# Inverting the gated-DeltaNet blocks in 16x16 pieces over 128 partitions, with one more merge on the tensor engine

## The chip, the cores and the metric

The kernel runs on one core of a Trainium2 chip. The metric is the device time of one execution in microseconds (us), the median of several runs of the same program. The engines of the core are named as the profile names them: PE (TensorE, the matmul engine) with PEld (its weight loads), DVE (VectorE), ACT (ScalarE), POOL (GpSimd) and SP (SyncE, which here only starts transfers). ACT also starts transfers; ACTq and SPq are the rows of those two queues.

## The reference, cut to what matters

One decoder layer over 2048 tokens of width 1024: a norm, an input projection that feeds three mixers (a convolution module, a gated DeltaNet with 4 heads of 64, differential attention), an output projection, and a SwiGLU network of width 2816. The part that the change touches is one triangular solve in the DeltaNet mixer, for every chunk of 64 tokens and every head:

```python
lower = jnp.where(strict, beta[..., None] * kk * decay, 0.0)
a_mat = lower + jnp.eye(c, dtype=jnp.float32)          # c = 64, unit lower triangular
...
sol = lax.linalg.triangular_solve(a_mat, rhs, left_side=True, lower=True, unit_diagonal=True)
u_c, w_c = sol[..., :dv], sol[..., dv:]
...
def step(state, inp):                                  # one step per chunk, in order
    v_new = u_i - jnp.einsum('bhcd,bhde->bhce', w_i, state)
    ...
```

There are 32 chunks and 4 heads, so 128 such 64x64 triangular matrices.

## The kernel before, in words

The 2048 tokens are worked on in four units of 512 (u = 0 to 3). A first phase runs, unit by unit, everything that needs the input projection. The order of its steps is written out by hand in one string: I is the DeltaNet's input projection with its short convolution, G the DeltaNet proper (`gdn_unit`), C the taps of the long convolution, L its norm, K and V the projections of attention, N the norm of the next unit, A the attention of unit 0. A planner then places the instructions of all engines with costs of its own and with priorities (`hp`); every engine then runs its own list strictly in that order. After the first phase come the attention of the other units, the output projection and the feed-forward network, in one long stream of matmuls. Large matmuls are done three times (`mm3`: high x high, high x low, low x high) and their weights go through three buffers `wp`, loaded by SP.

`gdn_unit` (L430) has 32 matrices in a unit (4 heads x 8 chunks). It forms the lower triangles L (L435 to L456), stores them to DRAM (`gL`, L457) and reads the two diagonal 32x32 blocks of each back with one block per partition: 64 partitions, 32x32 numbers each (`Lg`, L463). DVE then inverts all 64 blocks at once by substitution: 31 steps of two instructions, an outer product (L470) and a subtraction from the rows below (L472). The inverses `Tt` and their transposes go back to DRAM (`gT`, L474, L475) and are read again in the layout of the tokens: the transposes into the diagonal of `X64` (L480), the first block untransposed into `T1` (L483). Two rounds of small matmuls on PE make the 32x32 block beside the diagonal: `yp` (L490) and, after a copy on ACT (L495), `wp` (L500), which ACT writes into `X64` (L503). PE's fp32 matmul appears in the trace as two instructions, so that the 32 matmuls of `yp` in a unit are 64 instructions, and the same for `wp`. Then a scan over the 8 chunks of the unit (L528 to L581) uses `X64` at L522 and L542 and carries the state `Sbd` (L562) from chunk to chunk and from unit to unit. All of its accumulators and those of the merge share two PSUM banks, the tags "sc" and "o".

The transfers of `gL`, `Lg`, `gT`, `X64` and `T1` are all started by ACT. SP starts the loads of weights (L114, L118). A tile's tag names its place in memory: tiles of one tag follow each other in the same place. The pools p1 and gd end with the first phase, and the tiles of the feed-forward phase (pool `pa`) take over gd's place once all its tiles are done with, the last of them those of the scan of unit 3 and of a first part of the output projection (`hx`, L1016 to L1023).

Of the kernel before, what the change touches and what calls it, by code (L numbers as in the profile page):

```python
# [10 lines left out]
F32 = mybir.dt.float32  # L11
F32R = mybir.dt.float32r
AF = mybir.ActivationFunctionType
ALU = mybir.AluOpType
# [33 lines left out]
def body(ctx: ExitStack, tc: tile.TileContext, x, norm1_g, w_in, conv_dw_w, conv_dw_b,  # L48
# [16 lines left out]
    gL = [dram.tile([H, U, C], F32, name=f"gL{u}", tag=f"gL{u}") for u in range(NU)]  # L65
    gT = [dram.tile([2, 2, H, 8, 32, 32], F32, name=f"gT{u}", tag=f"gT{u}") for u in range(NU)]

# [5 lines left out]
    def cst(shape, name):  # L73
        return const.tile(shape, F32, name=name, tag=name)
# [172 lines left out]
    V.memset(Sbd, 0.0)  # L247
    X64 = cst([P, H, TU, C], "X64")
    V.memset(X64, 0.0)
    hist4 = cst([P, 6, 3], "hist4")  # L250
# [179 lines left out]
    def gdn_unit(u, qtok, sc):  # L430
        L, QKT = sc["L"], sc["QKT"]

        def qkh(tt):
            return qtok[:, tt, 0:512].rearrange("p (h d) -> p h d", d=C)
        for tt in range(TU):  # L435
# [10 lines left out]
            for hp in range(2):  # L446
# [8 lines left out]
                for d_, b in ((L, 0), (QKT, 1)):  # L455
                    V.tensor_tensor(d_[:, hp::2, tt, :], kv[:, :, b, :], d_[:, hp::2, tt, :], op=ALU.mult)  # L456
        nc.scalar.dma_start(gL[u].rearrange("h (t p) c -> p (h t) c", p=P), L.rearrange("p h t c -> p (h t) c"))  # L457

        Lg = gd.tile([64, 32, 32], F32, name=f"Lg{u}", tag="Lg")
        Tt = gd.tile([64, 32, 32], F32, name=f"Tt{u}", tag="Tt")  # L460
        for blk in range(2):
            b0 = blk * 32
            nc.scalar.dma_start(Lg[b0:b0 + 32], gL[u].rearrange("h (c r) s -> (h c) r s", c=8)[:, b0:b0 + 32, b0:b0 + 32])  # L463
        V.memset(Tt, 0.0)
        V.memset(Tt.rearrange("p a b -> p (a b)")[:, 0:1024:33], 1.0)
        for j in range(31):
            n = 31 - j
            tm = gd.tile([64, 256], F32, name=f"tm{u}_{j}", tag="tg")
            tv = tm[:, 0:n * (j + 1)].rearrange("p (a b) -> p a b", a=n)
            V.tensor_tensor(tv, Lg[:, j + 1:, j:j + 1].to_broadcast([64, n, j + 1]),  # L470
                            Tt[:, j:j + 1, 0:j + 1].to_broadcast([64, n, j + 1]), op=ALU.mult)
            V.tensor_tensor(Tt[:, j + 1:, 0:j + 1], Tt[:, j + 1:, 0:j + 1], tv, op=ALU.subtract)  # L472
        V.tensor_copy(Lg, Tt.rearrange("p a b -> p b a"))
        nc.scalar.dma_start(gT[u][0].rearrange("k h c a b -> (k h c) a b"), Tt)  # L474
        nc.scalar.dma_start(gT[u][1].rearrange("k h c a b -> (k h c) a b"), Lg)  # L475
        T1 = gd.tile([P, H, TU, 32], F32, name=f"T1_{u}", tag="Lg")
        for ch in range(2):
            for blk in range(2):
                r0 = ch * C + blk * 32
                nc.scalar.dma_start(  # L480
                    X64[r0:r0 + 32, :, :, blk * 32:blk * 32 + 32].rearrange("p h t c -> p (h t) c"),
                    gT[u][1, blk].rearrange("h (t c) s q -> c s (h t) q", c=2)[ch])
            nc.scalar.dma_start(T1[ch * C:ch * C + 32].rearrange("p h t c -> p (h t) c"),  # L483
                              gT[u][0, 0].rearrange("h (t c) s q -> c s (h t) q", c=2)[ch])

# [110 lines left out]
    def conv_ln(u, acc2):  # L596
# [22 lines left out]
        for ct in range(2):  # L619
            yl = acc2[:, ct, :]  # L620
            ty = gd.tile([P, U], F32, name=f"cy{u}_{ct}", tag="cm", bufs=CMB)
            A.activation(ty, yl, AF.Tanh)
            V.scalar_tensor_tensor(ty, ty, 1.0, yl, op0=ALU.add, op1=ALU.mult)
            nc.scalar.dma_start(yT[ct * P:(ct + 1) * P, u * U:(u + 1) * U], ty)
# [376 lines left out]
    hy = [q0[:, k] for k in range(3)] + [gd.tile([P, 2, U], F32R, name="hy3", tag="QKT", bufs=2)]  # L1001
    hx = Rot([P, U], F32, (gd, "Tt"), (gd, "Lg"), (gd, "L"))
    hyr = Rot([P, U], F32, (gd, "dd"), (gd, "tg"))
# [260 lines left out]
```

## Time and profile before

| | us |
|---|---|
| median of 3 runs | 2916.71 |
| lowest, highest of the runs | 2912.79, 2918.99 |
| the profiled execution | 2917.14 |
| its span in the trace | 2915.4 |

The profiled execution lies 0.43 us above the median of the runs, and 1.7 us of it lie outside the span. Sums are made against the profiled execution. PE is busy for 2800.1 us of the span, DVE for 1565.9, POOL for 1111.3 and ACT for 1050.0. A matmul that waits in PE's pipe counts as busy, so the distance between the starts of two matmuls says more than their length. The granted clock of PE is 1 at its higher level (2.4 GHz) and 0.5 at its lower (1.2 GHz); a value between them is a mean over a stretch that has both.

### The profile page before, as it was taken

Reading aid. Unit: us, or ns where it says so; the run is one execution under the profiler, and the core shown is the slowest. Engines: PE = TensorE matmul, PEld = TensorE weight load, DVE = VectorE, ACT = ScalarE, POOL = GpSimd, SP = SyncE. Lnnn points to the kernel's source line nnn. Section 1 sums busy time; section 2 is a strip of 40 time slices with the busy share of each in tenths; the row PEclk is TensorE's granted clock in tenths of the full one; section 3 lists DMA queues with packets and bytes.
Section 4 is the critical chain, followed back from the end, with each engine's and each line's share of the span. In section 5 each row is a group of like instructions: output and inputs, shape, how many; then the busy total and the mean of one; then the engine's idle time right before and its main releaser. Section 6 shows DMA issues by size and latency. Waiting matters only on the chain.

```text
span 2915.4 us, 39754 instructions
## 1 busy us (share of the span) xinstructions
PE 2800.1 (96%) x14673; PEld 2284.4 (78%) x14673; DVE 1565.9 (54%) x3443; ACT 1050.0 (36%) x2237; POOL 1111.3 (38%) x1021
## 2 busy tenths in 40 slices
PE   7979989999988999999998999999999999999998
PEld 6867777778776788887877888887878888888886
DVE  8976776877766765565566655541332222422223
ACT  4333223322154544444455434442332222322222
POOL 4421010001033444344455434444644444444543
PEclk9989999999988999999999999999999999999999
DMA  7784573654776544444366344324343333323332
GB/s 253 242 274 153 178 232 127 207 179 138 254 200 219 144 131 122 112 126 118 108 182 203 86 130 120 93 88 151 102 149 99 96 94 101 116 87 102 101 94 87
DMA packets 404064, 422.52 MB, mean 145 GB/s; under 512 B 46448, under 2 KB 326170, under 8 KB 392606
## 3 DMA queue, kind: packets, MB, share of 16 engines
q1 hardware_dynamic: 344222, 373.31, 41.8%
q10 hardware_dynamic: 59648, 46.67, 5.1%
q8 instruction: 116, 1.90, 0.3%
q14 instruction: 78, 0.64, 0.1%
HBM read 344.35 MB, written 75.56 MB: 144 GB/s over the span
## 4 chain that ended last, share of the span: by engine, by line
PE 80%; DVE 8%; DMA 6%; issue 2%; ACT 2%; POOL 1%; ACTq 0%; SPq 0%; POOLq 0%; DVEq 0%
PE pg L137 6%; PE pg L138 6%; PE pg L139 6%; PE pu L139 5%; PE pu L137 5%; PE pu L138 5%; PE pd L137 5%; PE pd L138 5%; PE pd L139 5%; PE s L784 3%; PE pt L830 2%; PE po L137 1%; PE po L138 1%; PE po L139 1%; PE ma L137 1%
## 5 line engine op out<-in xcount | busy, mean ns | idle before, releaser
L121 POOL TENSOR_TENSOR wp<-wr,wp 128x512 fp32r<-128x512 f32 (+1 forms) x666 | 906.7, 1386 | 865.4 <-ACT wp L120 847.9
L120 ACT CAST wp<-wr 128x512 fp32r<-128x512 f32 (+1 forms) x666 | 378.6, 617 | 871.5 <-PE pd L139 229.1
L137 PE MATMUL pd<-wp,ac 128*128 128x512 f32 x704 | 279.8, 400 | 9.2 <-DVE x L1154 7.6
L1154 DVE TENSOR_TENSOR x<-x,pd 128x512 f32<-128x512 f32 x192 | 130.4, 685 | 285.6 <-PE pd L139 285.2
L137 PE MATMUL pg<-h,wp 128*128 128x512 f32 x704 | 279.6, 397 | 3.4 <-ACT h L1075 1.7
L138 PE MATMUL pd<-wp,ac 128*128 128x512 f32 x704 | 277.1, 394 | 2.1 <-POOL wp L121 2.1
L139 PE MATMUL pd<-wp,ac 128*128 128x512 f32 x704 | 277.5, 394 | 1.5 <-DVE ac L1138 1.5
L139 PE MATMUL pu<-h,wp 128*128 128x512 f32 x704 | 278.4, 396 | 0.0
L139 PE MATMUL pg<-h,wp 128*128 128x512 f32 x704 | 278.3, 395 | 0.0
L137 PE MATMUL pu<-h,wp 128*128 128x512 f32 x704 | 277.3, 394 | 0.6 <-DVE ft L1135 0.6
L138 PE MATMUL pu<-h,wp 128*128 128x512 f32 x704 | 277.8, 395 | 0.0
L138 PE MATMUL pg<-h,wp 128*128 128x512 f32 x704 | 277.6, 394 | 0.0
L1134 DVE SCALAR_TENSOR_TENSOR ft<-ft,pg 128x512 f32<-128x512 f32 x88 | 60.4, 686 | 244.1 <-ACT ft L1133 244.1
L784 PE MATMUL s<-kk,qq 128*128 128x512 f32 (+3 forms) x576 | 171.6, 384 | 5.5 <-DVE mx L787 5.1
L593 DVE SCALAR_TENSOR_TENSOR cp<-hc,cwT,cp 128x512 f32<-128x512 f32 x232 | 173.2, 747 | 2.5
L137 PEld LDWEIGHTS pd<-wp,ac 128*128 128x128 f32 x704 | 132.7, 188 | 45.8 <-DVE x L1154 15.1
L137 PEld LDWEIGHTS pg<-h,wp 128*128 128x128 f32 x704 | 132.3, 188 | 36.2 <-ACT wp L120 5.4
L139 PEld LDWEIGHTS pd<-wp,ac 128*128 128x128 f32 x704 | 132.5, 188 | 31.7 <-DVE ac L1138 3.1
L138 PEld LDWEIGHTS pd<-wp,ac 128*128 128x128 f32 x704 | 132.8, 189 | 30.2 <-POOL wp L121 3.5
L137 PEld LDWEIGHTS pu<-h,wp 128*128 128x128 f32 x704 | 132.3, 188 | 30.0 <-ACT wp L120 1.0
L138 PEld LDWEIGHTS pu<-h,wp 128*128 128x128 f32 x704 | 132.3, 188 | 29.7
L138 PEld LDWEIGHTS pg<-h,wp 128*128 128x128 f32 x704 | 132.3, 188 | 28.8 <-DVE h L1076 0.2
(389 smaller groups left out, 5866.0 us busy)
## 6 DMA issues: line engine op xcount, KB each, us to landing
wr<-in_w_ffn_in_dram SPq DMA_DIRECT2D x176, 512.0 KB, 3.9
wp<-ws SPq DMA_DIRECT2D x66, 1024.0 KB, 5.8
wr<-in_w_ffn_out_dram SPq DMA_DIRECT2D x88, 512.0 KB, 3.5
ws<-wp SPq DMA_DIRECT2D x22, 1024.0 KB, 6.9
wr<-in_w_out_dram SPq DMA_DIRECT2D x44, 512.0 KB, 3.6
arena<-vs SPq DMA_DIRECT2D x80, 256.0 KB, 3.8
kk<-ks SPq DMA_DIRECT2D x64, 256.0 KB, 5.0
qq<-qs SPq DMA_DIRECT2D x96, 128.0 KB, 4.5
```

What stands on the lines that cost most here:

```text
L120: A.copy(w[:, 0, q], raw[:, q])
L121: G.tensor_tensor(w[:, 1, q], raw[:, q], w[:, 0, q].bitcast(F32), op=ALU.subtract)
L137: T.matmul(ps, lhsT=lh, rhs=rh, start=start, stop=False)
L138: T.matmul(ps, lhsT=lh, rhs=rl, start=False, stop=False)
L139: T.matmul(ps, lhsT=ll, rhs=rh, start=False, stop=stop)
L593: V.scalar_tensor_tensor(acc2[:, ct, :] if j == 30 else acc, hj, w, acc, op0=ALU.mult, op1=ALU.add)
L784: T.matmul(sp[:, 0:w], lhsT=qq[c][:, l, q0:q0 + P], rhs=kt_[x][c][:, k0:k0 + w], start=l == 0, stop=l == 1)
L830: T.transpose(pt[:, col:col + P], ptile[b][kt // 8][:, (kt % 8) * P:(kt % 8 + 1) * P], ident)
L1134: V.scalar_tensor_tensor(t_, t_, 1.0, pg, op0=ALU.add, op1=ALU.mult)
L1154: V.tensor_tensor(xs_, xs_, pd, op=ALU.add)
```

## The change

The blocks that are inverted by substitution become 16x16 and there are four for each matrix, so 128 for a unit: one for each partition. The substitution has 15 steps in place of 31. Two pairs of 16x16 inverses are then merged to 32x32 inverses by a new round on PE: `zp` (64 matmuls of 32x32x32 for a unit, over all four groups of 32 partitions in turn), a copy on ACT (`zm`), `vm` (64 matmuls) and `nm` (32 matmuls, the untransposed form of the first block for `T1`); ACT writes four strips of `vm` into `X64`, DVE makes `T1` in two subtractions. The old merge (`yp`, `wp`) follows as before. The blocks beside the 16x16 diagonal are read from `gL` into a new tile `L16` by four transfers on SP; the untransposed inverses come back from `gT` into a new tile `D16` by six transfers on SP; `Lg` is read by four transfers and `X64` by eight, on ACT. `X64` exists twice, for even and odd units, the even one in gd. To make room, `T1` moves to the tag "pr" of p1, the tile `ty` of the convolution's norm to the tag "cc" of p1, and `hx` takes the places of `X0` and `hc` in place of those of `Tt` and `Lg`.

```diff
@@ -63,7 +63,7 @@
     xp = dram.tile([U, D], F32, name="xp", tag="xp")
     zd = dram.tile([S, 256], F32, name="zd", tag="zd")
     gL = [dram.tile([H, U, C], F32, name=f"gL{u}", tag=f"gL{u}") for u in range(NU)]
-    gT = [dram.tile([2, 2, H, 8, 32, 32], F32, name=f"gT{u}", tag=f"gT{u}") for u in range(NU)]
+    gT = [dram.tile([2, 4, H, 8, 16, 16], F32, name=f"gT{u}", tag=f"gT{u}") for u in range(NU)]
 
 
     const = ctx.enter_context(tc.tile_pool(name="const", bufs=1))
@@ -245,8 +245,14 @@
     V.memset(ones, 1.0)
     Sbd = cst([P, 2, P], "Sbd")
     V.memset(Sbd, 0.0)
-    X64 = cst([P, H, TU, C], "X64")
-    V.memset(X64, 0.0)
+    XX = [gd.tile([P, H, TU, C], F32, name="X0", tag="X0"), cst([P, H, TU, C], "X1")]
+    for X64 in XX:
+        V.memset(X64, 0.0)
+
+    D16 = gd.tile([P, H, TU, 32], F32, name="D16", tag="D16")
+    V.memset(D16, 0.0)
+    L16 = gd.tile([P, H, TU, 32], F32, name="L16", tag="L16")
+    V.memset(L16, 0.0)
     hist4 = cst([P, 6, 3], "hist4")
     V.memset(hist4, 0.0)
     hist30 = cst([P, 2, 30], "hist30")
@@ -428,7 +434,7 @@
         sc.update(c1=c1, c2=c2, c3=c3)
 
     def gdn_unit(u, qtok, sc):
-        L, QKT = sc["L"], sc["QKT"]
+        L, QKT, X64 = sc["L"], sc["QKT"], XX[u % 2]
 
         def qkh(tt):
             return qtok[:, tt, 0:512].rearrange("p (h d) -> p h d", d=C)
@@ -455,33 +461,67 @@
                 for d_, b in ((L, 0), (QKT, 1)):
                     V.tensor_tensor(d_[:, hp::2, tt, :], kv[:, :, b, :], d_[:, hp::2, tt, :], op=ALU.mult)
         nc.scalar.dma_start(gL[u].rearrange("h (t p) c -> p (h t) c", p=P), L.rearrange("p h t c -> p (h t) c"))
-
-        Lg = gd.tile([64, 32, 32], F32, name=f"Lg{u}", tag="Lg")
-        Tt = gd.tile([64, 32, 32], F32, name=f"Tt{u}", tag="Tt")
-        for blk in range(2):
-            b0 = blk * 32
-            nc.scalar.dma_start(Lg[b0:b0 + 32], gL[u].rearrange("h (c r) s -> (h c) r s", c=8)[:, b0:b0 + 32, b0:b0 + 32])
+        for ch in range(2):
+            for blk in range(2):
+                r0 = blk * 32
+                nc.sync.dma_start(
+                    L16[ch * C + r0 + 16:ch * C + r0 + 32, :, :, 0:16].rearrange("p h t c -> p (h t) c"),
+                    gL[u].rearrange("h (t c r) s -> c r (h t) s", c=2, r=C)[ch, r0 + 16:r0 + 32, :, r0:r0 + 16])
+
+        Lg = gd.tile([P, 16, 16], F32, name=f"Lg{u}", tag="Lg")
+        Tt = gd.tile([P, 16, 16], F32, name=f"Tt{u}", tag="Tt")
+        for k in range(4):
+            b0 = k * 16
+            nc.scalar.dma_start(Lg[k * 32:k * 32 + 32],
+                                gL[u].rearrange("h (c r) s -> (h c) r s", c=8)[:, b0:b0 + 16, b0:b0 + 16])
         V.memset(Tt, 0.0)
-        V.memset(Tt.rearrange("p a b -> p (a b)")[:, 0:1024:33], 1.0)
-        for j in range(31):
-            n = 31 - j
-            tm = gd.tile([64, 256], F32, name=f"tm{u}_{j}", tag="tg")
+        V.memset(Tt.rearrange("p a b -> p (a b)")[:, 0:256:17], 1.0)
+        for j in range(15):
+            n = 15 - j
+            tm = gd.tile([P, 64], F32, name=f"tm{u}_{j}", tag="tg")
             tv = tm[:, 0:n * (j + 1)].rearrange("p (a b) -> p a b", a=n)
-            V.tensor_tensor(tv, Lg[:, j + 1:, j:j + 1].to_broadcast([64, n, j + 1]),
-                            Tt[:, j:j + 1, 0:j + 1].to_broadcast([64, n, j + 1]), op=ALU.mult)
+            V.tensor_tensor(tv, Lg[:, j + 1:, j:j + 1].to_broadcast([P, n, j + 1]),
+                            Tt[:, j:j + 1, 0:j + 1].to_broadcast([P, n, j + 1]), op=ALU.mult)
             V.tensor_tensor(Tt[:, j + 1:, 0:j + 1], Tt[:, j + 1:, 0:j + 1], tv, op=ALU.subtract)
         V.tensor_copy(Lg, Tt.rearrange("p a b -> p b a"))
         nc.scalar.dma_start(gT[u][0].rearrange("k h c a b -> (k h c) a b"), Tt)
         nc.scalar.dma_start(gT[u][1].rearrange("k h c a b -> (k h c) a b"), Lg)
-        T1 = gd.tile([P, H, TU, 32], F32, name=f"T1_{u}", tag="Lg")
         for ch in range(2):
-            for blk in range(2):
-                r0 = ch * C + blk * 32
-                nc.scalar.dma_start(
-                    X64[r0:r0 + 32, :, :, blk * 32:blk * 32 + 32].rearrange("p h t c -> p (h t) c"),
-                    gT[u][1, blk].rearrange("h (t c) s q -> c s (h t) q", c=2)[ch])
-            nc.scalar.dma_start(T1[ch * C:ch * C + 32].rearrange("p h t c -> p (h t) c"),
-                              gT[u][0, 0].rearrange("h (t c) s q -> c s (h t) q", c=2)[ch])
+            for k in range(4):
+                r0 = ch * C + k * 16
+                for dst, m, c0 in ((X64, 1, k * 16), (D16, 0, k % 2 * 16)):
+                    if m or k < 3:
+                        (nc.scalar if m else nc.sync).dma_start(
+                            dst[r0:r0 + 16, :, :, c0:c0 + 16].rearrange("p h t c -> p (h t) c"),
+                            gT[u][m, k].rearrange("h (t c) s q -> c s (h t) q", c=2)[ch])
+
+        zp = sct_(f"zp{u}")
+        for th in range(TU * H):
+            for r0 in range(0, P, 32):
+                T.matmul(zp[r0:r0 + 32, th * 32:th * 32 + 32], lhsT=L16[r0:r0 + 32, th % H, th // H, :],
+                         rhs=X64[r0:r0 + 32, th % H, th // H, r0 % C:r0 % C + 32], start=th == 0,
+                         stop=th == TU * H - 1, skip_group_check=True)
+        zs_ = gd.tile([P, TU * H, 32], F32, name=f"zm{u}", tag="dd")
+        A.copy(zs_, zp.rearrange("p (h x) -> p h x", x=32))
+        vp_ = sct_(f"vm{u}")
+        for th in range(TU * H):
+            for r0 in range(0, P, 32):
+                T.matmul(vp_[r0:r0 + 32, th * 32:th * 32 + 32], lhsT=D16[r0:r0 + 32, th % H, th // H, :],
+                         rhs=zs_[r0:r0 + 32, th, :], start=th == 0, stop=th == TU * H - 1, skip_group_check=True)
+        np_ = ps_sc.tile([P, 512], F32, name=f"nm{u}", tag="o")
+        for th in range(TU * H):
+            for r0 in (0, C):
+                T.matmul(np_[r0:r0 + 32, th * 32:th * 32 + 32], lhsT=zs_[r0:r0 + 32, th, :],
+                         rhs=D16[r0:r0 + 32, th % H, th // H, :], start=th == 0, stop=th == TU * H - 1,
+                         skip_group_check=True)
+        T1 = p1.tile([P, H, TU, 32], F32, name=f"T1_{u}", tag="pr")
+        for r0 in range(0, P, 32):
+            A.mul(X64[r0:r0 + 16, :, :, r0 % C + 16:r0 % C + 32].rearrange("p h t x -> p t h x"),
+                  vp_[r0:r0 + 16, :].rearrange("p (t h x) -> p t h x", t=TU, h=H)[:, :, :, 16:32], -1.0)
+        for r0 in (0, C):
+            V.tensor_tensor(T1[r0:r0 + 32].rearrange("p h t x -> p t h x"),
+                            D16[r0:r0 + 32].rearrange("p h t x -> p t h x"),
+                            np_[r0:r0 + 32, :].rearrange("p (t h x) -> p t h x", t=TU, h=H), op=ALU.subtract)
 
         yp = sct_(f"yp{u}")
         for ch in range(2):
@@ -618,7 +658,7 @@
                              scale=cwT[:, ct, 32:33])
         for ct in range(2):
             yl = acc2[:, ct, :]
-            ty = gd.tile([P, U], F32, name=f"cy{u}_{ct}", tag="cm", bufs=CMB)
+            ty = p1.tile([P, U], F32, name=f"cy{u}_{ct}", tag="cc")
             A.activation(ty, yl, AF.Tanh)
             V.scalar_tensor_tensor(ty, ty, 1.0, yl, op0=ALU.add, op1=ALU.mult)
             nc.scalar.dma_start(yT[ct * P:(ct + 1) * P, u * U:(u + 1) * U], ty)
@@ -999,7 +1039,7 @@
 
     q0 = gd.tile([P, 3, 2, U], F32R, name="hy012", tag="qtok", bufs=2)
     hy = [q0[:, k] for k in range(3)] + [gd.tile([P, 2, U], F32R, name="hy3", tag="QKT", bufs=2)]
-    hx = Rot([P, U], F32, (gd, "Tt"), (gd, "Lg"), (gd, "L"))
+    hx = Rot([P, U], F32, (gd, "X0"), (gd, "hc"), (gd, "L"))
     hyr = Rot([P, U], F32, (gd, "dd"), (gd, "tg"))
     hp1 = bank((ps_mm, "mm1"))
     for k in range(4):
```

## Rows read from the trace of the kernel before

**Rows 1.** The page: part 1 (busy time, share of the span, instructions of each engine) and the line PE of part 2 (busy tenths in 40 slices of 73 us).

```profile
PE 2800.1 (96%) x14673; PEld 2284.4 (78%) x14673; DVE 1565.9 (54%) x3443; ACT 1050.0 (36%) x2237; POOL 1111.3 (38%) x1021
...
PE   7979989999988999999998999999999999999998
```

**Rows 2.** Busy time of each engine in windows of the first phase and the start of the next (start:end, length, busy time and instructions of PE, PEld, DVE, ACT, POOL, then the granted clock, the share of the DMA engines and GB/s).

```profile
100.00:200.00 100.00, 84.53 (x496) 71.56 (x495) 90.94 (x199) 33.21 (x77) 32.24 (x28) 0.90 0.77 264
...
400.00:500.00 100.00, 92.25 (x622) 76.76 (x623) 64.60 (x173) 30.15 (x65) 8.79 (x9) 0.94 0.48 161
...
700.00:800.00 100.00, 99.96 (x663) 82.07 (x662) 74.55 (x189) 20.10 (x47) 11.40 (x13) 1.00 0.74 239
...
900.00:1000.00 100.00, 88.83 (x438) 69.32 (x437) 75.88 (x198) 51.83 (x120) 46.94 (x52) 0.90 0.67 198
```

**Rows 3.** What PE waited for between 100 and 1000 us (total us, times, longest).

```profile
PE ma L137 <- DVE ql L711: 13.7, 3, 8.2
...
PE mq L137 <- DMA wp<-ws: 4.1, 1, 4.1
```

**Rows 4.** Groups of instructions by line in the window 0 to 1000 us (busy us, mean ns of one, idle before).

```profile
L472 DVE TENSOR_TENSOR Tt<-Tt,tm 64x31 f32<-64x31 f32 (+15 forms) x124 | 43.2, 348 | 1.6
L470 DVE TENSOR_TENSOR tm<-Lg,Tt 64x31 f32<-64x31 f32 (+15 forms) x124 | 42.5, 342 | 3.8 <-DMA Lg<-gL 2.2
...
L728 DVE TENSOR_TENSOR ve<-mw,ve 128x512 fp32r<-128x512 f32 x16 | 11.0, 686 | 16.3 <-DMA vs<-ve 7.4 <-ACT ve L727 4.6 <-DMA ks<-ql 4.3
...
L324 ACT COPY ut<-mq 128x512 f32<-128x512 f32 x24 | 14.0, 584 | 12.0 <-PE mq L139 9.7 <-DMA gT<-Lg 2.3
```

**Rows 5.** DVE in order of time, single instructions of the substitution (start, length).

```profile
199.15 1.12 DVE L473 COPY Lg<-Tt 64x1024 f32<-64x1024 f32 x1
...
723.13 0.20 DVE L470 TENSOR_TENSOR tm<-Lg,Tt 64x31 f32<-64x31 f32 x1 [1.95 <-DMA Lg<-gL]
...
723.86 0.21 DVE L472 TENSOR_TENSOR Tt<-Tt,tm 64x60 f32<-64x60 f32 x1
```

**Rows 6.** The chain that ended last, in order of time: runs of small fp32 matmuls (start, length of the run, instructions). L490 and L500 use 32x32 blocks of PE's array, one block after another of the same place; L542 the same with 64x64 and 64 columns; L522 likewise, but its neighbours write to two different halves of the output partitions in turn.

```profile
212.92 1.12 PE yp L490 x32
...
224.02 2.04 PE wp L500 x64
...
229.31 0.38 PE kt L522 x8
...
238.60 0.60 PE vp L542 x8
```

**Rows 7.** PE in order of time around waits in units 0 and 2 (start, length, in brackets the idle time before and what ended it).

```profile
169.68 0.77 PE L137 MATMUL ma<-ht,wp 128*128 128x512 f32 x1 [8.19 <-DVE ql L711]
170.25 0.63 PE L138 MATMUL ma<-ht,wp 128*128 128x512 f32 x1
...
173.99 0.39 PE L138 MATMUL ma<-ht,wp 128*128 128x512 f32 x1
174.22 0.40 PE L139 MATMUL ma<-ht,wp 128*128 128x512 f32 x1
...
182.23 0.76 PE L137 MATMUL ma<-ht,wp 128*128 128x512 f32 x1 [3.98 <-DVE ql L711]
...
642.18 1.91 PE L490 MATMUL yp<-X,L 32*32 32x32 f32 x32 [2.36 <-DMA X<-gT]
```

**Rows 8.** Busy time of DVE with the instructions of line L470 alone, in two windows (start:end, length, busy, instructions, clock, DMA).

```profile
161.49:169.68 8.19, 1.45 (x4) 0.63 0.94 321
171.00:182.23 11.23, 3.65 (x10) 0.80 0.48 173
```

**Rows 9.** The same windows with the instructions of line L472 alone.

```profile
161.49:169.68 8.19, 1.18 (x3) 0.63 0.94 321
171.00:182.23 11.23, 4.25 (x9) 0.80 0.48 173
```

**Rows 10.** What the SP queue waited for between 0 and 850 us.

```profile
SPq L114 <- PE ma L139: 143.2, 21, 10.4
...
SPq L114 <- DMA T<-gT: 11.6, 2, 10.0
```

**Rows 11.** Transfers between 0 and 850 us (issuing queue, count, KB each, median us from issue to landing).

```profile
wp<-ws SPq DMA_DIRECT2D x66, 1024.0 KB, 5.8
...
yT<-cy ACTq DMA_DIRECT2D x6, 256.0 KB, 6.1
```

**Rows 12.** PE in order of time in the merge and the start of the scan of unit 3.

```profile
801.34 1.17 PE L490 MATMUL yp<-X,L 32*32 32x32 f32 x32 [0.77 <-DMA X<-gT]
...
809.90 2.11 PE L500 MATMUL wp<-ys,T 32*32 32x32 f32 x64
...
816.42 0.45 PE L522 MATMUL kt<-X,prg 64*64 64x64 f32 x8
```

**Rows 13.** DVE in order of time: the end of the substitution and of the scan of unit 3.

```profile
787.45 1.11 DVE L473 COPY Lg<-Tt 64x1024 f32<-64x1024 f32 x1
...
921.09 0.89 DVE L573 TENSOR_TENSOR os<-os,zr 128x256 f32<-128x256 f32 x1
```

**Rows 14.** The SP queue in order of time: the last stores of the first part of the output projection, and the first loads into pa.

```profile
914.88 6.63 SPq L1023 DMA_DIRECT2D xp<-hx  x2
...
927.63 0.93 SPq L1085 DMA_DIRECT2D yr<-yT  x2
```

## The prediction

> **What bounds the kernel now.** I read the page first: PE is busy for 96% of the span, and in 38 of 40 slices for eight tenths or more [rows 1]. DVE, whose work the change cuts, is at 54% [rows 1]. So the default view is that only PE's own list counts: what is added there is paid, and what is taken from DVE is worth only the time for which PE stood still behind DVE. The second view, windows of 100 us, shows where that can be [rows 2]: from 100 to 200 us PE has 84.5 us of work, a mean clock of 0.90, and DVE is at 91%. Later windows leave less: 92.3 us from 400 to 500, 100.0 from 700 to 800 although DVE is at 75% there, and 88.8 from 900 to 1000, where the feed-forward phase begins. The third view, PE's waits, names the largest one that DVE ends: 13.7 us for `ql` (L711), all of it in unit 0 [rows 3, 7]. The substitution stands in that place: `ql` is behind the taps of the convolution and the steps L470 and L472 in DVE's list.
>
> **Part 1, the substitution.** Before: 42.5 us and 43.2 us in 124 instructions each [rows 4], 21.4 us for a unit, and the copy L473 with 1.12 us [rows 5]; a memset of `Tt` of the same size comes on top. After: 15 steps of two instructions on at most 64 numbers a partition. The rows at 31 and 60 numbers are 0.20 and 0.21 us [rows 5], so 30 x 0.2 = 6.0 us; more partitions cost nothing in these rows' terms, because all partitions run side by side. The copy of 256 numbers instead of 1024 is at most a third, 0.4 us. The two subtractions for `T1` read PSUM with 512 numbers a partition: 0.69 us each by L728 [rows 4], 1.4 us. The balance is 22.5 - 7.8 = 14.7 us of DVE for a unit, 59 us in all.
>
> What that is worth is read from the stalls. In unit 0 PE stands still for 8.19 us until 169.68 and for 3.98 us until 182.23 [rows 7]. After each, some ten matmuls follow at the lower clock level: their rows are 0.63 us long, and 0.39 us (one each 0.23 us) once the clock is up [rows 7]; that is about 0.2 us each, 2 us a stall. The most that can be won is 8.2 + 4.0 + 4.4 = 16.6 us. But in the first stall the substitution has only 1.45 + 1.18 = 2.6 us of DVE's time, and before the second 3.65 + 4.25 = 7.9 us [rows 8, 9]; the rest is taps and norm. A half of it goes away with the change (the early steps stay as long), so I take 2.5 us off the first stall, all of the second and its slow matmuls: 2.5 + 4.0 + 2.4, **about -9 us**. In unit 1 the waits are 4.1 us for a weight load [rows 3] and others for transfers; DVE is not what comes last, and I take -2 us for it. Unit 2's wait ahead of `yp`, 2.4 us, is for a transfer [rows 7], and in unit 3 the window from 700 to 800 is full [rows 2].
>
> **Part 2, the matmuls that are added.** 64 + 64 + 32 = 160 a unit, which are 320 instructions by the way the trace counts fp32, 1280 in all. Nothing in the old list goes away. The same shape runs in 1.12/32 = 35 ns (`yp`) and 2.04/64 = 32 ns (`wp`) for each instruction when one follows the other in one block of the array [rows 6]. The new ones go round four blocks with different input and different output partitions. The trace has one nearest row: L522 alternates between two output halves and takes 0.38/8 = 48 ns, where L542, the same shape without alternation, takes 0.60/8 = 75 ns, a ratio of 0.63 [rows 6]. So: no overlap at all, 1280 x 35 ns = 45 us; four blocks fully beside each other, a quarter of 34 ns, 11 us; the ratio of the nearest row, 22 ns, **+28 us**, which I take. Below 11 us I see nothing: PE works its list in order, and the instructions are all new.
>
> **Part 3, the chain of one unit.** The new round adds zp, a copy on ACT (0.58 us by L324 [rows 4]), vm and nm, four strips on ACT, bounded by the same 0.58 us each, and T1. ACT gets 2.9 us more a unit at 36% busy [rows 1]; at nothing, hidden behind dense matmuls; without that cover 12 us in all. The length of the chain matters only in unit 3, as the scan of each unit needs the state of the one before. There the substitution runs from 723.1 to 787.5 [rows 5, 13], stretched by the taps between its steps; the merge is on PE from 801.3 to 812.0 and the scan starts at 816.4 [rows 12]. With 30 instructions for 62 the stretch of 64 us would be 31, 33 us less; another round like the old one costs 12 us back; the scan could start 21 us earlier. The scan ends at about 922 [rows 13], and the first load into `pa` follows at 927.6 [rows 14]. But the last stores of `hx`, which hold the same memory, end at 921.5 too [rows 14], and they are not moved. So of 21 us I credit **-5 us**; none and 15 us are the ends, the latter being most of the 11.2 us of idle time and the clock of 0.90 from 900 to 1000 [rows 2].
>
> **Part 4, transfers and memory.** Ten of the new transfers stand on SP, among the loads of weights, and wait there for `gL` and `gT` to land; behind them in SP's list are the next `wp` loads, for which PE waits. Three `wp` buffers cover two pieces of 24 matmuls at 0.23 us, 11 us, of which the load itself needs 5.8 [rows 7, 11]: a hold of up to about 5 us is free. Before, SP already waited 11.6 us for a small load of the merge [rows 10] and PE 4.1 us for weights [rows 3]. I take **+3 us**, between nothing and 30 (below). `ty` in the tag "cc" holds the only buffer of the short convolution until its store has landed, 6.1 us [rows 11], twice a unit; two `ut` buffers and two PSUM banks stand before PE, so nothing, and up to 12 us a unit if the planner lets the two alternate. The second `X64` takes away a wait for the last scan, which is late only once the chain is shorter. `hx` in other places: nothing, those are free by then.
>
> A rule that speaks against the change. No row of the kernel before alternates between input partitions; the nearest, L522, alternates between output halves alone and shows a gain [rows 6]. The Trainium skill, TensorEngine Tiling (Array Packing), Restrictions and Gotchas, says: "Different row tiles cannot access same PSUM bank simultaneously". All four blocks of `zp` write one bank, so by it they would run one after another, for 45 us, and the sum below would be 2949. The same page's Theoretical Speedup gives up to four times for dimensions of 32 or less; by that the sum would be 2915. No run here shows either.
>
> **Sum.** 2917.1 + 28 - 9 - 2 - 5 + 3 = 2932 us.
>
> **The rivals.**
> Faster: the matmuls run beside each other (11 us), and the DVE relief is paid in full: -16.6 in unit 0, -4 in unit 1, -15 at the start of the feed-forward phase. 2917 + 11 - 36 + 3 = 2895, and 2900 with a little less. For it speaks DVE at 91% in the window that PE loses most [rows 2]; against it that taps, not substitution, fill the first stall [rows 8, 9]. 30%.
> Serial: the added matmuls cost 35 ns each, 45 us instead of 28, with the other terms as above: 2949. It is decided by the distance between the starts of neighbours in `zp`, at 30 ns or more. This is what the sentence of the Trainium skill, TensorEngine Tiling (Array Packing), on PSUM banks (Restrictions and Gotchas) would do. 16%.
> SP: its list is held for 10 us in each unit, 5 us past the cover, with 2 us of slow matmuls after each stall: 4 x 7 = 28 us in place of 3, 2957. It decides from a hold of about 5 us. 5%.
> No change: the cost stays small (15 us) and the relief near its middle (18 us), or the planner moves the work so that the two cancel: 2917, within 0.2%. 17%.
> The forecast itself: 32%, between 2923 and 2941.
>
> **How the numbers follow.** A measurement of this kernel can tell about 0.2% from no change, 6 us. Slower are the forecast, the serial case and the SP case, 0.53; the same 0.17; faster 0.30. Two in ten may be left out: the range goes from 2895 (the faster case's working out; about 0.1 lies below) to 2960 (just past the SP case; about 0.1 lies above).
>
> **What would show it.** Right: PE's instructions up by 1280, `zp` at 20 to 25 ns for each instruction, the lines of the substitution at 24 us in all, PE's wait for `ql` at 5 us or less, the window 100 to 200 nearer to full. Wrong: `zp` at 9 or 35 ns; a wait of PE for `wp` loads with SP held by `L16` or `D16`; the first load into `pa` well ahead of 927 us. The sum would be wrong above all if the planner places the steps of the first phase so differently that waits appear or vanish far from the merge.

## The result, and the profile after

The changed kernel takes 2948.36 us (median of 4 runs, 2937.52 to 2958.42), the kernel before 2917.85 us (4 runs, 2912.79 to 2919.34): a ratio of 1.0108, with a 95% interval of 1.0081 to 1.0134. It is slower by some 31 us; 2932 us had been forecast. The profiled execution of the changed kernel is its slowest, with a span of 2956.7 us against 2915.4, so the accounts below explain 41 us, of which the median run has about 10 less.

The page of the changed kernel: part 1, the line PE of part 2, and from part 3 one of the two queues that bring instructions (packets, MB, share).

```profile
PE 2819.8 (95%) x15953; PEld 2297.3 (78%) x15953; DVE 1520.4 (51%) x3326; ACT 1057.4 (36%) x2257; POOL 1107.4 (37%) x1021
...
PE   7979989999898899999999999999999999999998
...
q8 instruction: 126, 2.06, 0.3%
```

PE has 1280 instructions more, as forecast, but only 19.7 us more of busy time [rows 1]. DVE has 45.5 us less.

A cut that can be compared is the first transpose for the norm of the feed-forward phase (`x3t`; L1071 before, L1111 after). Up to it PE executes 5769 instructions before and 7051 after, which is the same work to within two instructions and the 1280 new ones. It starts at 974.8 us before and at 1015.4 us after, 40.6 us later; what follows takes 1940.6 and 1941.3 us. So the whole loss lies ahead of this cut. The window up to the cut in the kernel before, then windows of the changed kernel (columns as in [rows 2]):

```profile
0.00:974.80 974.80, 902.13 (x5769) 730.06 (x5769) 733.15 (x1828) 327.69 (x782) 213.11 (x227) 0.95 0.64 204
```

```profile
0.00:1015.40 1015.40, 923.86 (x7051) 743.38 (x7052) 689.93 (x1716) 335.35 (x803) 212.82 (x227) 0.95 0.61 194
100.00:200.00 100.00, 84.90 (x485) 70.74 (x485) 75.91 (x167) 32.67 (x76) 33.00 (x29) 0.88 0.78 251
950.00:975.00 25.00, 13.67 (x56) 10.60 (x55) 7.26 (x22) 6.74 (x18) 9.24 (x10) 0.67 0.92 303
```

The kernel before has 902.1 us of PE's work in its 974.8 us, so 72.7 us of idle time. After, it is 923.9 us and 91.5 us: 21.7 us more work and 18.9 us more idle time. From 100 to 200 us DVE went from 90.9 to 75.9 us, and PE from 84.5 to 84.9 [rows 2]. In this window DVE's relief did not reach PE.

The matmuls of the new round, in groups by line (busy us, mean ns of one, idle before):

```profile
L501 PE MATMUL zp<-X,L 32*32 32x32 f32 x512 | 7.6, 195 | 5.1 <-issue 5.1
L514 PE MATMUL nm<-D,zm 32*32 32x32 f32 x256 | 5.4, 194 | 6.0 <-issue 6.0
L509 PE MATMUL vm<-zm,D 32*32 32x32 f32 x512 | 5.2, 193 | 0.0
```

They are 18.2 us of PE's time, and 11.1 us of idle time that the profile calls "issue": PE waited for nothing that it shows. No such time stands in the kernel before. PE in order of time, where the longest but one of these gaps lies:

```profile
200.52 1.19 PE L501 MATMUL zp<-X,L 32*32 32x32 f32 x111
205.49 0.42 PE L501 MATMUL zp<-X,L 32*32 32x32 f32 x11 [3.78 <-issue]
205.84 0.80 PE L137 MATMUL ma<-ht,wp 128*128 128x512 f32 x1
206.43 0.63 PE L138 MATMUL ma<-ht,wp 128*128 128x512 f32 x1
```

111 instructions of one group pass in 1.19 us, 11 ns each. Then PE stands still in the middle of the group for 3.8 us, and the matmuls behind it run at 0.63 us each, the length that they have at the lower of the clock's two levels [rows 7]: the granted clock is 1.00 from 200 to 201.7 us and 0.50 from 205.5 to 210.

What else PE waited for up to 1100 us, and DVE's lines of the substitution with the subtraction for `T1`:

```profile
PE ma L137 <- DVE nss L288: 7.7, 1, 7.7
PE mw L137 <- DVE ve L768: 6.9, 1, 6.9
...
PE to L895 <- DVE arena L913: 4.5, 1, 4.5
PE mq L137 <- DMA wp<-ws: 3.9, 2, 3.4
PE po L137 <- ACT yt L1126: 3.9, 1, 3.9
```

```profile
L485 DVE TENSOR_TENSOR Tt<-Tt,tm 128x15 f32<-128x15 f32 (+7 forms) x60 | 13.1, 219 | 1.0
L483 DVE TENSOR_TENSOR tm<-Lg,Tt 128x15 f32<-128x15 f32 (+7 forms) x60 | 12.6, 210 | 2.7 <-DMA Lg<-gL 1.9
...
L522 DVE TENSOR_TENSOR T<-D,nm 32x512 f32<-32x512 f32 x8 | 5.4, 678 | 10.2 <-PE nm L514 10.1
```

The substitution fell from 85.7 us to 25.7 us [rows 4], where 24 had been forecast, and the subtraction costs 5.4 us, where 5.6 had been. On these lines DVE's part of the forecast was right to 2 us. Of the 59 us that the forecast took off DVE in all, 45.5 show in its busy time. PE got next to nothing of it.

### The profile page after: what moved, and what is told of

It is laid out like the page before. It is cut to its first block, busy times and chain, and to the rows that moved or that the text cites. A ratio compares the mean times of both kernels' runs of the same rounds, so it can differ in the third digit from the quotient of the medians.

```text
span 2956.7 us, 42319 instructions
## 1 busy us (share of the span) xinstructions
PE 2819.8 (95%) x15953; PEld 2297.3 (78%) x15953; DVE 1520.4 (51%) x3326; ACT 1057.4 (36%) x2257; POOL 1107.4 (37%) x1021
## 4 chain that ended last, share of the span: by engine, by line
PE 67%; DMA 4%; DVE 4%; issue 2%; ACT 1%; POOL 1%; ACTq 0%; SPq 0%; POOLq 0%; DVEq 0%
PE pg L137 6%; PE pg L138 5%; PE pg L139 5%; PE pu L139 5%; PE pu L137 5%; PE pu L138 5%; PE pd L137 5%; PE pd L138 5%; PE pd L139 5%; PE s L824 3%; PE pt L870 2%; PE po L137 1%; PE po L138 1%; PE po L139 1%; PE po L884 1%
## 5 line engine op out<-in xcount | busy, mean ns | idle before, releaser
L121 POOL TENSOR_TENSOR wp<-wr,wp 128x512 fp32r<-128x512 f32 (+1 forms) x666 | 902.1, 1379 | 867.8 <-ACT wp L120 855.7
```

Source lines behind the costliest of these rows:

```text
L121: G.tensor_tensor(w[:, 1, q], raw[:, q], w[:, 0, q].bitcast(F32), op=ALU.subtract)
```

## The experiments

Two theories stood against each other. Theory A: the added matmuls and their gaps cost about 30 us, and DVE's relief is worth little. Theory B: the matmuls are cheap, and the moved tiles, the transfers on SP or the waits that they make cost the time. Ratios are to runs of the kernel before on the same chip, with 95% intervals.

**Without the new merge (a_nomerge).** From the change zp, vm and nm go:

```diff
-        zp = sct_(f"zp{u}")
...
-        np_ = ps_sc.tile([P, 512], F32, name=f"nm{u}", tag="o")
...
         T1 = p1.tile([P, H, TU, 32], F32, name=f"T1_{u}", tag="pr")
-        for r0 in range(0, P, 32):
-            A.mul(X64[r0:r0 + 16, :, :, r0 % C + 16:r0 % C + 32].rearrange("p h t x -> p t h x"),
...
+        for r0 in (0, C):
+            V.tensor_copy(T1[r0:r0 + 32], D16[r0:r0 + 32])
```

> The changed kernel without zp, vm, nm and their copies: T1 is a copy of D16 and the 16x16 block beside the diagonal of X64 stays zero, so the result of the merge is left out; all transfers and the short substitution stay. Theory A (the added matmuls are what costs: 18 us of PE time, 11 us of gaps in which PE's sequencer waits for nothing that shows, and 3 us of slow clock behind them): 2948 - 32 = 2916, between 2908 and 2924, no such gaps left. Rival B (the new transfers, the moved tiles and other waits cost): it stays at 2938 or more. Rival C (DVE's relief is worth 16 us as forecast for the first phase, and the merge costs still more): 2905 or less.

Measured: 2929.05 us, 1.0040 (1.0025 to 1.0055). No gaps are left, and the queue q8 carries 116 packets again:

```profile
q8 instruction: 116, 1.90, 0.3%
```

About 19 us come back, not 32, and 12 us stay lost although DVE is relieved and no matmul is added. Between theory A and B; C is out.

**The matmuls alone (b_matmuls).** Into the kernel before, ahead of `yp` (the same again as vm, and over the blocks 0 and C as nm):

```diff
+        zp = sct_(f"zp{u}")
+        for th in range(TU * H):
+            for r0 in range(0, P, 32):
+                T.matmul(zp[r0:r0 + 32, th * 32:th * 32 + 32], lhsT=L[r0:r0 + 32, th % H, th // H, 0:32],
+                         rhs=X64[r0:r0 + 32, th % H, th // H, r0 % C:r0 % C + 32], start=th == 0,
+                         stop=th == TU * H - 1, skip_group_check=True)
...
```

> The kernel before with 160 extra 32x32 matmuls a unit in the order of the change (four blocks in turn), on data that lie there anyway, ahead of yp; nobody reads what they give. Theory A: 1280 instructions at about 10 ns, 13 to 18 us, and gaps of some 3 us each in half of the units, 11 us: 2917 + 27 = 2944, between 2935 and 2950. Rival B (the matmuls are cheap, the loss is made by the transfers and moved tiles): 2917 + 15 = 2932 or less and no gaps. The forecast's price of 22 ns: 2945 without any gap.

Measured: 2964.46 us, 1.0161 (1.0133 to 1.0188), above all three expectations. Groups by line:

```profile
L501 PE MATMUL nm<-X,L 32*32 32x32 f32 x256 | 8.5, 204 | 4.0 <-issue 4.0
L489 PE MATMUL zp<-X,L 32*32 32x32 f32 x512 | 8.4, 198 | 3.1 <-DMA X<-gT 2.8 <-issue 0.3
L495 PE MATMUL vm<-X,L 32*32 32x32 f32 x512 | 6.5, 200 | 9.4 <-issue 9.3
```

23.4 us of work and 13.6 us of gaps, 37 us where 27 had been expected; the gaps come back in a kernel that has nothing else of the change. So they belong to these matmuls. The other 10 us or so are not in a row of the merge.

The two ways to price the merge do not agree: 19 us by what comes back in a_nomerge, some 47 by b_matmuls. By the same numbers the change, with its shorter substitution, is some 16 us faster than b_matmuls, while b_half below, with the shorter substitution alone, is slower than the kernel before. The effects do not add, and the profiles do not show why: the changed kernel (2958 us) and b_matmuls (2964 us) reach the cut `x3t` within 1 us of each other.

**One block after another (a_serial), and two at a time (a_pairs).** In a_serial the loops of zp, vm and nm are turned:

```diff
-        for th in range(TU * H):
-            for r0 in range(0, P, 32):
+        for r0 in range(0, P, 32):
+            for th in range(TU * H):
```

> The changed kernel with the loops of zp, vm and nm turned: all 32 instructions of one block of the array, then the next block. Theory A (10 ns an instruction because blocks run side by side; the gaps come from the list being emptied faster than it is filled): 32 to 35 ns an instruction as for yp and wp, 43 us in place of 18, and the 11 us of gaps gone: 2948 + 14 = 2962, between 2955 and 2970. If the gaps have nothing to do with the pace of the list: 2973. Rival B (price of the matmuls does not decide): 2948 within 6.

In a_pairs zp and vm go over the blocks in two pairs:

```diff
-        for th in range(TU * H):
-            for r0 in range(0, P, 32):
+        for th, r0 in [(th, r0) for pr_ in ((0, 32), (64, 96)) for th in range(TU * H) for r0 in pr_]:
```

> The changed kernel with zp and vm going round two blocks of the array at a time in place of four. Theory A (the gaps come from the pace at which the list is emptied): about 18 ns an instruction for zp and vm, 1024 x 18 + 5 = 23 us in place of 18, and gaps of 5 us or less in place of 11: 2948 within 6. If the gaps do not depend on the pace: 11 us stay and the time is 2953 or more.

Measured: a_serial 2977.3 us, 1.0207 (1.0185 to 1.0230); a_pairs 2945.23 us, 1.0091 (1.0072 to 1.0109). The groups of a_serial, then those of a_pairs:

```profile
L501 PE MATMUL zp<-X,L 32*32 32x32 f32 x512 | 18.7, 201 | 3.0 <-DMA X<-gT 3.0
L509 PE MATMUL vm<-zm,D 32*32 32x32 f32 x512 | 17.4, 198 | 0.0
L514 PE MATMUL nm<-D,zm 32*32 32x32 f32 x256 | 12.7, 227 | 1.7 <-issue 1.7
```

```profile
L500 PE MATMUL zp<-X,L 32*32 32x32 f32 x512 | 9.6, 192 | 0.0
L507 PE MATMUL vm<-zm,D 32*32 32x32 f32 x512 | 8.7, 192 | 0.0
L512 PE MATMUL nm<-D,zm 32*32 32x32 f32 x256 | 5.5, 194 | 3.9 <-issue 3.9
```

Divide busy time by count: `vm` takes 34 ns an instruction with one block at a time, 17 with two, 10 with four (5.2 us for 512). Blocks with different input and output partitions run beside each other into one PSUM bank, two of them fully and four at 3.4 times the pace of one. The gaps go the other way, 1.7, 3.9 and 11.1 us: the faster the instructions pass, the more PE stands still. Single profiles scatter, and the order holds: the other kernels with four blocks in turn have 5.2 (a_onex_ty), 6.7 (a_actq) and 13.6 us (b_matmuls), the other one with two has 4.3 (a_pairs_early, below). a_serial came out 15 us above what theory A gave, of which 6 us are that its merge takes 48.8 us and not 43.

**The transfers on ACT (a_actq).** All ten transfers into L16 and D16 go to the other queue:

```diff
-                nc.sync.dma_start(
+                nc.scalar.dma_start(
                     L16[ch * C + r0 + 16:ch * C + r0 + 32, :, :, 0:16].rearrange("p h t c -> p (h t) c"),
...
-                        (nc.scalar if m else nc.sync).dma_start(
+                        nc.scalar.dma_start(
```

> The changed kernel with the ten transfers a unit into L16 and D16 started by ACT in place of SP. If SP's holds delay the loads of weights (rival B, SP): 10 us or more come back, 2938 or less. Theory A: 2948 within 6, and the gaps in zp and nm stay.

Measured: 2956.0 us, 1.0123 (1.0098 to 1.0148). Nothing comes back, and 6.7 us of gaps stay. SP did wait in the changed kernel:

```profile
SPq L467 <- DMA gL<-L: 12.3, 2, 10.2
```

but PE's waits for weights did not grow: 4.2 us for `wp` in all, where the kernel before has 7.0 (4.1 of it in [rows 3]). The hold stays under its cover. Theory B's form with SP is out.

**The moved tiles (b_ty, a_onex_ty).** In b_ty, `ty` alone is moved in the kernel before:

```diff
-            ty = gd.tile([P, U], F32, name=f"cy{u}_{ct}", tag="cm", bufs=CMB)
+            ty = p1.tile([P, U], F32, name=f"cy{u}_{ct}", tag="cc")
```

> The kernel before with the tile ty of the long convolution moved into the one buffer of the short convolution, as in the change. If this move makes the 13 us that the change costs without its merge: 2925 or more, with a wait of DVE or ACT for the store out of cy. If not: 2916 within 6.

In a_onex_ty the change has one X64 again, and `ty` in its old place:

```diff
-    XX = [gd.tile([P, H, TU, C], F32, name="X0", tag="X0"), cst([P, H, TU, C], "X1")]
+    XX = [cst([P, H, TU, C], "X1")] * 2
...
-    hx = Rot([P, U], F32, (gd, "X0"), (gd, "hc"), (gd, "L"))
+    hx = Rot([P, U], F32, (gd, "D16"), (gd, "hc"), (gd, "L"))
```

> The changed kernel with one X64 for all units, and ty back in its old place (hx takes the place of D16 for that of X0). If the moved tiles make what the change costs beside its matmuls: about 13 us less, 2935. If they do not: 2948 within 6. If the second copy of X64 was a help: 2955 or more.

Measured: b_ty 2922.59 us, 1.0010 (1.0000 to 1.0020); a_onex_ty 2950.41 us, 1.0112 (1.0095 to 1.0129). The move of `ty` costs nothing or up to 6 us, and two copies of X64 are neither help nor harm that can be told. Theory B's form with these two tiles is out; the new place of `T1` was not tested by itself.

**DVE's relief alone (b_half).** In the kernel before the substitution is cut short, to the rows up to 15:

```diff
-        for j in range(31):
-            n = 31 - j
+        for j in range(15):
+            n = 15 - j
...
-            V.tensor_tensor(tv, Lg[:, j + 1:, j:j + 1].to_broadcast([64, n, j + 1]),
+            V.tensor_tensor(tv, Lg[:, j + 1:16, j:j + 1].to_broadcast([64, n, j + 1]),
...
```

> The kernel before with the substitution cut to the first 15 of its 31 steps on the first 16 rows (the other rows are left out, so the inverses are not complete); everything else stays, no matmul is added. It gives DVE the relief of the change alone. The forecast's credit (9 + 2 + 5 us, PE's stalls behind DVE and the start of the feed-forward phase): 2916 - 16 = 2900, between 2893 and 2906. Rival (what DVE no longer does is not what PE waits for; the same stalls stay behind ACT's and PE's own part of the norm): 2916 within 6. Third (a planner's new order costs by itself what the change without its merge cost, 13 us): 2925 or more.

Measured: 2925.19 us, 1.0035 (1.0016 to 1.0054). With 61 us less on DVE's two lines and nothing added, the time does not fall; it rises by 5 to 16 us. Its windows up to `x3t` and from 100 to 200 us, and its largest waits of PE:

```profile
0.00:976.70 976.70, 898.33 (x5752) 723.34 (x5752) 681.93 (x1695) 324.14 (x778) 208.57 (x226) 0.96 0.64 203
100.00:200.00 100.00, 85.78 (x556) 72.41 (x555) 77.29 (x169) 33.37 (x78) 31.91 (x28) 0.91 0.80 262
```

```profile
PE po L137 <- ACT yt L1086: 12.4, 2, 9.4
PE ntp L292 <- DVE x L286: 9.0, 1, 9.0
PE ma L137 <- DVE nss L282: 7.4, 1, 7.4
PE ma L137 <- DVE ql L711: 4.2, 2, 2.8
```

In this kernel the credit of 16 us for DVE does not come, with no matmul to hide it. From 160 to 200 us PE waits for DVE for 10.2 us (7.4 and 2.8), where it was 12.2 before and is 10.2 in the changed kernel. Something does come in the first phase: up to 500 us PE has stood still for 44.9 us, against 51.0 before. It is lost behind, above all from 900 to 950 us (PE's work in the kernel before, then in b_half):

```profile
900.00:950.00 50.00, 42.09 (x210) 32.17 (x209) 34.58 (x97) 21.10 (x49) 20.41 (x25) 0.86 0.69 222
```

```profile
900.00:950.00 50.00, 35.03 (x149) 26.20 (x148) 22.70 (x69) 17.71 (x41) 20.74 (x22) 0.86 0.76 242
```

The scan of unit 3 ends at 886.7 us here, 35.7 us earlier than before (922.5, the end of the last `ot`), and the first load into `pa` starts at 921.9, only 5.7 us earlier than in [rows 14]; PE then waits 12.4 us for `yt`, which is made from that load.

**The next link (b_half_early, b_early, b_128_early, a_pairs_early).** A new theory: the stores of `hx`, whose weights come behind the last projection of unit 3, hold the memory of `pa`. All four write that block (hy, hx and hp, here a function) earlier:

```diff
+        if step == "V3":
+            first_out()
```

b_128_early spreads the 32x32 substitution over 128 partitions besides: each block's columns in two halves, `m = min(j + 1, 16)` columns a step.

> The kernel before with the substitution cut to 15 steps as in b_half (the other rows are left out) and with the first part of the output projection (hy, hx, hp) written ahead of step V3 in place of behind the last step. Theory (DVE's relief ends the scan 36 us earlier, but the feed-forward phase waits for the stores of hx, which stand behind the last projection of unit 3 and did not move): with hx early the wait of po for yt (12.4 us in b_half) goes, the first load into pa comes before 905 us, and the time falls from 2925 to 2912, between 2906 and 2917. Rival (the relief is lost elsewhere, hx is not what ends last): 2925 within 6.

> The kernel before with hy, hx and hp written ahead of step V3; a control. In the kernel before the stores of hx and the last scan end within 1 us of each other, so hx alone should be worth nothing much: 2917 within 6. If the place of hx is worth as much here as in b_half_early, 2905 or less, the credit there is not DVE's.

> The kernel before with the 32x32 substitution spread over 128 partitions (each block's two halves of columns side by side; 31 steps, at most 256 numbers each, no added matmul), and hx early. DVE's lines of the substitution fall from 86 us to 55 or 60. Theory: about two thirds of what b_half_early gains, 2914, between 2906 and 2918. Rival (relief is worth nothing here): 2917 or more.

> The change with zp and vm in pairs of blocks (as a_pairs) and hx early. Theory: the tail's extra idle time (9 us more than before between the last scan and the first transpose of the feed-forward phase) goes, the matmuls and their gaps stay: 2945 - 10 = 2935, between 2928 and 2940. Rival (the tail follows the matmuls, not hx): 2945 within 5.

Measured: b_half_early 2933.23 us, 1.0044 (1.0028 to 1.0061); b_early 2937.73, 1.0066 (1.0050 to 1.0081); b_128_early 2939.55, 1.0066 (1.0049 to 1.0082); a_pairs_early 2952.56, 1.0114 (1.0095 to 1.0131). The theory falls. In b_half_early the last store starts at 859 us, the wait for `yt` shrinks to 2.0 us and the scan ends at 907 us, but SP starts the first load into `pa` later than before, and it waited for the attention of unit 0 meanwhile (SP in order of time, its waits from 890 to 965 us, PE's largest new wait):

```profile
859.08 0.54 SPq L960 DMA_DIRECT2D xp<-hx  x1
...
942.70 1.18 SPq L1089 DMA_DIRECT2D yr<-yT  x2
```

```profile
SPq L884 <- PE t L870: 10.5, 1, 10.5
```

```profile
PE po L843 <- DMA arena<-vs: 6.2, 1, 6.2
```

The matmuls of `hp` were what PE had to do beside that attention; written early, they are used up. b_128_early measures something else than was meant: the cap of 16 columns takes only 5456 numbers a substitution down to 4776, its two lines on DVE stay at 85.1 us, and it repeats b_early. No version beats the kernel before; a_pairs is level with the change.

## Why the prediction was right in sign and half in size

The account at the cut `x3t`, in us. PE's work and idle time are from the windows up to the cut, the merge and the gaps from the groups by line and the waits. The first six have the same old work to within 5 instructions of PE, the last three 17 to 35 less.

| kernel | cut | PE's work | of it zp, vm, nm | PE idle | of it "issue" | other work | other idle |
|---|---|---|---|---|---|---|---|
| before | 974.8 | 902.1 | 0 | 72.7 | 0 | 902.1 | 72.7 |
| b_ty | 979.5 | 900.1 | 0 | 79.4 | 0 | 900.1 | 79.4 |
| the change | 1015.4 | 923.9 | 18.2 | 91.5 | 11.1 | 905.7 | 80.4 |
| a_pairs | 1002.0 | 926.5 | 23.8 | 75.5 | 3.9 | 902.7 | 71.6 |
| a_serial | 1032.5 | 957.6 | 48.8 | 74.9 | 1.7 | 908.8 | 73.2 |
| a_onex_ty | 1008.7 | 928.3 | 19.9 | 80.4 | 5.2 | 908.4 | 75.2 |
| b_half | 976.7 | 898.3 | 0 | 78.4 | 0 | 898.3 | 78.4 |
| a_nomerge | 989.7 | 908.8 | 0 | 80.9 | 0 | 908.8 | 80.9 |
| b_matmuls | 1014.6 | 923.5 | 23.4 | 91.1 | 13.6 | 900.1 | 77.5 |

- **PE's own list counts: right.** The added instructions are paid, in every kernel that has them.
- **The matmuls, +28 us: right as a sum, by luck, and wrong as a mechanism.** 22 ns an instruction had been taken; they run at 14 ns (18.2 us for 1280), and 11.1 us of gaps come on top, 29.3 us in the profile of the change. The lower end of 11 us for blocks fully side by side was close for the work and left the gaps out. The step "below 11 us I see nothing" had a cost on the other side that it did not look for: that at a pace of 10 ns PE stands still within the group.
- **The rule on PSUM banks does not set the pace of these blocks.** By the Trainium skill, TensorEngine Tiling (Array Packing), Restrictions and Gotchas, different row tiles cannot access one bank at a time. Read as the prediction read it, that the blocks run one after another, it does not agree with `vm` at 34, 17 and 10 ns with one, two and four row tiles, each writing its own partitions of one bank. The Trainium skill, TensorEngine Tiling (Array Packing), Theoretical Speedup, has up to four times for a dimension of 32 or less; the trace agrees (34 / 10 = 3.4). The serial rival gave nearly the time that came, 2949, and by the wrong mechanism: a_serial shows what it would have cost.
- **DVE's relief, -9 and -2 us: the step that failed.** From 160 to 200 us PE waited 12.2 us for DVE before and 10.2 us after (7.7 and 2.5), and 10.2 us in b_half; 2 us came off where 6.5 had been credited, with 2.4 more for the clock, which is 0.88 from 100 to 200 us where it was 0.90. DVE in order of time in the changed kernel, and one line of ACT between, show why:

```profile
166.94 0.35 DVE L309 SCALAR_TENSOR_TENSOR ht<-ntp,g1T,ht 128x128 fp32r<-128x128 f32 x1 [2.81 <-ACT ht L308]
...
173.85 0.68 DVE L751 SCALAR_TENSOR_TENSOR ql<-ma,qh 128x512 fp32r<-128x512 f32 x1
...
184.59 0.61 DVE L309 SCALAR_TENSOR_TENSOR ht<-ntp,g1T,ht 128x128 fp32r<-128x128 f32 x2 [3.25 <-ACT ht L308]
...
185.65 0.68 DVE L751 SCALAR_TENSOR_TENSOR ql<-ma,qh 128x512 fp32r<-128x512 f32 x1
```

```profile
166.53 0.37 ACT L308 ACTIVATE ht<-ntp,g1T 128x128 fp32r<-128x128 f32 x1 [4.08 <-PE ntp L298]
```

  DVE waits for ACT's half of the norm ahead of both `ql`, and ACT for transposes on PE, which stand in PE's list among the matmuls that wait for `ql`. What was taken from DVE became DVE's own idle time. That the taps fill the first stall had been said; that the rest of the stall closes a ring over PE and ACT had not. In unit 1 PE's wait for `ve` is 6.9 us where it was 2.4. b_half got some 6 us of PE's idle time back by 500 us, and its tail lost them; what the relief is worth beside the merge stays open, as the effects do not add.
- **The tail, -5 us: wrong in sign.** The scan of unit 3 ends at 940.9 us after the change (922.5 before), and from the start of the last transpose of its output (`ot`) to `x3t` it is 74.8 us where it was 52.6; from 950 to 975 us PE has 13.7 us of work. It is not the scan that the next phase waits for. The last matmul of `hp` starts at 954.3 us where it was 918.8, late with PE's whole list (40.6 us at the cut), and the first load into `pa` follows the last store of `hx`, 35 us later than in [rows 14]:

```profile
959.39 0.32 SPq L1063 DMA_DIRECT2D xp<-hx  x1
...
962.66 0.96 SPq L1125 DMA_DIRECT2D yr<-yT  x2
```

  b_half shows that even a scan 36 us earlier does not bring `x3t` forward. That the stores of `hx` hold the memory had been written down, and 5 us were credited all the same; b_half_early shows the attention of unit 0 behind them.
- **SP, +3 us, and the moved tiles, nothing: right** within what a_actq, b_ty and a_onex_ty can tell. One reason given for it was not: the places of `hx` are not free by then. SP holds the load of `hx` into the place of `hc` until the taps have read it, which ends at 815.1 us:

```profile
SPq L1056 <- DVE ca L633: 14.9, 1, 14.9
```

  No wait of PE behind it shows its price. The prediction also left out the memsets of `X0`, `D16` and `L16`, 1.9 us of DVE ahead of the first norm; PE's first wait is 9.7 us where it was 8.8.
- **What is left.** The last two columns of the table scatter over 10 us each without regard to DVE: the kernels with the short substitution have 71.6 to 80.9 us of other idle time, those with the long one 72.7 to 79.4. b_ty changes no work at all and differs by 6.7. Each edit makes the planner lay out the first phase anew. That this makes the 12 us of a_nomerge and the 10 us of b_half is argued, not shown: no run held the order fixed while one cost changed. It is also open why a run of the changed kernel can differ from another by 21 us; the gaps, 5.2 to 13.6 us in profiles of like merges, may be a part of it.

The gaps: that they come with dense runs of small instructions, and grow with the pace, is shown (four, two and one block at a time; gone in a_nomerge, there in b_matmuls). One of 1.2 us stands in `yp` in b_half_early, which has no added matmul. That PE then waits for its own instructions is argued from the packets of q8: 10 more of them, 16 KB each, for 2560 entries more (1280 matmuls with their weight loads), so 256 entries a packet. By this estimate, at 10 ns a matmul a packet's 128 matmuls are gone in 1.3 us; at 0.23 us, the pace of the large ones [rows 7], they last 29 us.

## What to carry to other kernels

Ask of a busy engine not how full it is but what its relief would leave as the next thing late: leave its work out in a run of its own, before something else is added to pay for it. On PE many small matmuls on different blocks of the array cost little more than a third of their serial time (18 us for 49), but in a dense run of them PE can stand still without a wait that the profile shows; going round two blocks in place of four lost 6 us of work and won 7 us of gaps against the profile of the change. And where a planner lays out the order, differences of some 10 us between two kernels are read as the effect of an edit only with a control that changes no work, as b_ty does. Two prices of one part that disagree, as those of the merge here, say that the prices do not add.

## What the runs showed of the hardware that was not expected

- Four 32x32 blocks with different input and output partitions run beside each other into one PSUM bank: 34, 17 and 10 ns an instruction of `vm` for one, two and four (a_serial, a_pairs, the change).
- PE stands still within dense runs of small fp32 matmuls, for up to 5.4 us (the longest in b_matmuls), with no wait in the profile. That it has outrun the supply of its instructions is argued. The Trainium skill, Runtime: NRT & Kernel Launch, Instruction fetch mechanics, has it that instructions come in blocks of 256 and that the cost of a new block is mostly hidden. The trace agrees with the block (10 packets for 2560 entries); if the gaps are the fetch, it is not hidden at this pace, but no row names what PE waited for.
- The long gaps cost twice: the large matmuls behind the one at 201.7 us ran at 0.63 us in place of 0.39 for some 5 us. Behind the gaps of 3.8 and 4.3 us the granted clock was 0.50; behind those of 1.3 and 1.7 us it stayed at 1.00.
